# A hybrid SSD and attention layer: decay matrices by one maximum and biased exponentials, group-norm inverse roots on one row through DRAM

## Chip, cores and metric

The kernel runs on one core of one Trainium2 chip. The metric is device time in microseconds (us), as the median of several executions. Of a run with a profile, the profiled execution has a time of its own, and a span: the time from its first to its last recorded instruction. Engines are TensorE (PE), VectorE (DVE), ScalarE (ACT), GpSimd (POOL) and SyncE (SP, which here only issues transfers).

## What is computed

One inference step of one decoder layer for a prompt of 512 tokens and 8 samples of 8 new tokens each, 576 columns in all, with model width 2048. One input projection feeds two branches: a Mamba-2 mixer (causal convolution, chunked scan with decays, a SiLU gate and a grouped RMS norm) and sliding-window attention. Two gated output projections, a last projection and a final norm follow. The change touches the mixer's decay matrix and its grouped norm. For each of 8 groups of 8 heads and each chunk of 128 tokens, with `acs` the running sum of dt times A (A is negative):

```
L[s, t] = exp(acs[t] - acs[s])   for s <= t, else 0
y       = (C B^T * L) x + state part + D x
g       = y * silu(z)
out     = g * rsqrt(mean over the group's 512 channels of g*g + eps) * w
```

The kernel keeps columns as tokens and partitions as channels, so the mean over channels is a sum over partitions, taken by a matmul with a matrix of ones: each of its 128 result rows is the same.

## The kernel before

Every projection is made of **columns**: 128 output channels by 576 tokens, over 16 blocks of 128 inputs. Weights and inputs are split in a high and a low float32r part, and three products are summed (`step` in `run_main`, line 333): 16 x 3 x 2 = 96 matmuls of 128x288 for a column. The weights of half a column arrive as one 128x1024 tile (`raw`, line 68, on SP's queue), ScalarE copies the high part (`wh`, line 75), and VectorE subtracts the low part (`wl`, line 76). A column's sum stands in PSUM; two such buffers exist, so a third column can only start when the first has been copied out by its `take` function.

The mixer is worked off in 8 groups, each of six convolution columns and one mix column. `take_conv` copies a finished column to SBUF with three ScalarE copies (lines 809 to 811, tile `craw`), and queues `conv_job`: a scaled copy (`cacc`, 825), three multiply-adds on VectorE (827), two silu passes (829, 830) and the copy of the convolution state (`co`, 836). `take_mix` (1096) applies a sigmoid to a mix column. With the last x column of a group, `ssd_job(g)` is queued (872 to 978). It forms the decay matrices with `lmat` (855 to 866), multiplies them by C B^T (870), forms the scaled inputs `xe`, `xd` (900) with their high part `xh` (903, ScalarE) and low part `xl` (904, POOL), runs four chunks and then the sample tokens (`ssd_sample`), and ends with the gate and the grouped norm: the squares are summed on POOL into `tot` (957, 959), `tot` is split in `th` (963, ScalarE) and `tl` (964, POOL), the matrix of ones sums over partitions (969), ScalarE takes the root (970), VectorE the reciprocal (971) and four multiplications (975), and SP stores `y_d` (977).

```
        for s in range(2):
            ps = bank()
            for i, t_ in enumerate((th, tl)):
                ten.matmul(ps[:, :TH], ones, t_[:, s * TH:(s + 1) * TH], start=i == 0, stop=i == 1)
            act.activation(sqr[:, s * TH:(s + 1) * TH], ps[:, :TH], AF.Sqrt, bias=eps, scale=1.0 / 512)
        vec.reciprocal(sqr, sqr)
```

The jobs are Python generators. After each block of a column, `pump` runs the next step of the queued jobs, and `wait(n)` lets n such steps pass. That gives the order in which the program is written. The order in which each engine executes is then set by a scheduler that runs ahead of time, on estimated durations: so an edit in one place can move instructions in others. On the chip each engine works off its own list in that fixed order and waits for what an instruction needs.

After the mixer, the attention branch's output is read back (`stg` from `o_d`, line 1242, SP), split by ScalarE and VectorE (`ah`, `al`, 1250 and 1251), and the columns of its output projection follow. In between, `fw` (1318) and `res` (1289) are loaded.

Of the kernel before, what the change touches and what calls it, by code (L numbers as in the profile page):

```python
# [10 lines left out]
F32 = mybir.dt.float32  # L11
F32R = mybir.dt.float32r
AF = mybir.ActivationFunctionType
ALU = mybir.AluOpType
PSUM = bass.MemoryType.PSUM

P = 128
# [5 lines left out]
NS = NB * NQ  # L23
T = NP_TOK + NS
TH = T // 2
DI = 4096
H = 64
G = 8
# [27 lines left out]
def AP(t, off, dims):  # L56
    return bass.AP(t.tensor, t.offset + off, [list(d) for d in dims])
# [23 lines left out]
def hybrid(ctx, tc, x_prompt, x_sample, cache_k, cache_v, state_conv, state_ssm, norm_w, w_in, conv_w,  # L81
# [5 lines left out]
    ten, vec, act, pool, sync = nc.tensor, nc.vector, nc.scalar, nc.gpsimd, nc.sync  # L87
# [18 lines left out]
    def scratch(shape, name):  # L106
        return dram.tile(shape, F32, tag=name, name=name)
# [10 lines left out]
    xb_d = scratch([D // 2, TH], "xb_d")  # L118
    oh_d = scratch([HEADS * BL], "oh_d")
    ea_d = scratch([H, T], "ea_d")  # L120
    acs_d = scratch([H, T], "acs_d")
    e4_d = scratch([H, 4], "e4_d")
    e8_d = scratch([H, 8], "e8_d")

    def pers_tile(shape, name):
        return pers.tile(shape, F32, tag=name, name=name)
# [7 lines left out]
    eps = pers_tile([P, 1], "eps")  # L134
    sinkb = pers_tile([P, HEADS], "sinkb")
    sinks_s = pers_tile([P, 4], "sinks_s")
    dt_n = pers_tile([P, 5, H], "dt_n")
    dtd_n = pers_tile([P, 5, H], "dtd_n")
    acs_n = pers_tile([P, 5, H], "acs_n")
    cd_b = pers_tile([P, H, 4], "cd_b")  # L140
    dec_s = pers_tile([P, 32, 8], "dec_s")
    ones = pers.tile([P, P], F32R, tag="ones", name="ones")
# [22 lines left out]
    for b in order:  # L165
        if b in (0, 1):
            c0 = OFF_MA + b * P
# [87 lines left out]
    now = {}  # L255
# [45 lines left out]
    def wait(n):  # L301
        for _ in range(n):
            yield
# [441 lines left out]
    def dt_job(dtT, bt):  # L745
        x_, s, s2, p_, rst = (t[:H] for t in (dtT, cten("s"), cten("s2"), cten("p"), cten("rst")))
        sync.dma_start(out=rst, in_=c_reset)

        act.activation(s, x_, AF.Abs)
        act.activation(s, s, AF.Exp, scale=-1.0)  # L750
        tc.keep_in_program_order(act.activation(bt[:, 1:2], bt[:, 1:2], AF.Exp))
        vec.tensor_scalar(out=p_, in0=s, scalar1=2.0, scalar2=None, op0=ALU.add)
        vec.reciprocal(p_, p_)
        vec.tensor_tensor(out=s, in0=s, in1=p_, op=ALU.mult)
        vec.tensor_tensor(out=s2, in0=s, in1=s, op=ALU.mult)
        vec.tensor_scalar(out=p_, in0=s2, scalar1=2.0 / 17.0, scalar2=None, op0=ALU.mult)
        for n in (15, 13, 11, 9, 7, 5, 3):
            vec.scalar_tensor_tensor(out=p_, in0=p_, scalar=2.0 / n, in1=s2, op0=ALU.add, op1=ALU.mult)
        vec.scalar_tensor_tensor(out=p_, in0=p_, scalar=2.0, in1=s, op0=ALU.add, op1=ALU.mult)
        vec.scalar_tensor_tensor(out=x_, in0=x_, scalar=0.0, in1=p_, op0=ALU.max, op1=ALU.add)  # L760
        yield

        vec.tensor_scalar(out=s, in0=x_, scalar1=bt[:, 1:2], scalar2=-1.0, op0=ALU.mult, op1=ALU.mult)
        vec.tensor_tensor_scan(out=s2, data0=rst, data1=s, initial=0.0, op0=ALU.mult, op1=ALU.add)
        sync.dma_start(out=acs_d, in_=s2)
        act.activation(p_, s2, AF.Exp)
        sync.dma_start(out=ea_d, in_=p_)
        e4 = now["s"].tile([H, 4], F32, tag="e4", name="e4", bufs=1)
        e8 = now["s"].tile([H, 8], F32, tag="e8", name="e8", bufs=1)
        vec.tensor_copy(e4, p_[:, 0:512].rearrange("p (c l) -> p c l", l=P)[:, :, P - 1])  # L770
        vec.tensor_copy(e8, p_[:, 512:T].rearrange("p (b q) -> p b q", q=8)[:, :, 7])
        sync.dma_start(out=e4_d, in_=e4)
        sync.dma_start(out=e8_d, in_=e8)

        for lo, hi, n in ((0, 512, P), (512, T, 8)):
            v = s2[:, lo:hi].rearrange("p (c l) -> p c l", l=n)
            o = s[:, lo:hi].rearrange("p (c l) -> p c l", l=n)
            vec.tensor_tensor(out=o, in0=v[:, :, n - 1:n].to_broadcast([H, (hi - lo) // n, n]), in1=v,
                              op=ALU.subtract)
        act.activation(s, s, AF.Exp)  # L780
        vec.tensor_tensor(out=s, in0=s, in1=x_, op=ALU.mult)
        yield from wait(14)
        for srcT, dst in ((x_, dt_n), (s, dtd_n), (s2, acs_n)):
            ps = bank()
            for b in range(4):
                ten.transpose(ps[:, b * H:(b + 1) * H], srcT[:, b * P:(b + 1) * P], ident[:H, :H])
            ten.transpose(ps[:NS, 4 * H:5 * H], srcT[:, 512:T], ident[:H, :H])
            vec.tensor_copy(dst[:, 0:4, :], ps[:, 0:4 * H].rearrange("p (b h) -> p b h", h=H))
            vec.tensor_copy(dst[:NS, 4, :], ps[:NS, 4 * H:5 * H])
            yield  # L790
        sync.dma_start(out=cd_b, in_=AP(e4_d, 0, [[0, P], [1, 4 * H]]))
        eb = kten([P, 512], "eb")
        sync.dma_start(out=eb, in_=AP(e8_d, 0, [[0, P], [1, 8 * H]]))
        for hf in range(2):
            pl = slice(64 * hf, 64 * hf + 64)
            pool.tensor_copy(dec_s[pl], eb[pl].rearrange("p (t h b) -> p t h b", h=2, b=8)[:, :, hf, :])
        yield
# [57 lines left out]
    def lmat(g, c0, n, blk, rows):  # L855
        out = []
        for q in range(2):
            l_ = kten([P, 4, P], "L")
            sync.dma_start(out=l_[:rows, :, :n], in_=AP(acs_d, (8 * g + 4 * q) * T + c0, [[0, rows], [T, 4], [1, n]]))
            for i in range(4):  # L860
                h = 8 * g + 4 * q + i
                vec.tensor_scalar(out=l_[:rows, i, :n], in0=l_[:rows, i, :n], scalar1=acs_n[:rows, blk, h:h + 1],  # L862
                                  scalar2=0.0, op0=ALU.subtract, op1=ALU.min)
            act.activation(l_[:rows, :, :n], l_[:rows, :, :n], AF.Exp)  # L864
            out.append(l_)
        return out

# [5 lines left out]
    def ssd_job(g):  # L873
# [5 lines left out]
        ps = bank([P, 4, P])  # L879
# [5 lines left out]
        ps = bank([P, 4, P])  # L885
# [7 lines left out]
        for c in range(4):  # L893
# [5 lines left out]
            for o_, w_ in ((xe, dtd_n), (xd, dt_n)):  # L899
                vec.tensor_tensor(out=o_.rearrange("p (h d) -> p h d", d=64), in0=px.rearrange("p (h d) -> p h d", d=64),  # L900
                                  in1=w_[:, c, 8 * g:8 * g + 8].unsqueeze(2).to_broadcast([P, 8, 64]), op=ALU.mult)
# [12 lines left out]
            ps = bank()  # L914
# [3 lines left out]
            if c:  # L918
                vec.tensor_tensor(out=sn.rearrange("p (h d) -> p h d", d=64), in0=st.rearrange("p (h d) -> p h d", d=64),
                                  in1=cd_b[:, 8 * g:8 * g + 8, c:c + 1].to_broadcast([P, 8, 64]), op=ALU.mult)  # L920
# [15 lines left out]
            for t in range(4):  # L936
                vec.scalar_tensor_tensor(out=xs[t][:, cs], in0=xs[t][:, cs], scalar=dsk[:, 4 * g + t:4 * g + t + 1],
                                         in1=src[:, t, :], op0=ALU.mult, op1=ALU.add)
            yield from wait(2)
        ps = bank([P, 4, P])  # L940
# [22 lines left out]
        act.activation(th, tot, AF.Copy)  # L963
        pool.tensor_tensor(out=tl, in0=tot, in1=th, op=ALU.subtract)
        yield from wait(8)
        for s in range(2):
            ps = bank()
            for i, t_ in enumerate((th, tl)):
                ten.matmul(ps[:, :TH], ones, t_[:, s * TH:(s + 1) * TH], start=i == 0, stop=i == 1)
            act.activation(sqr[:, s * TH:(s + 1) * TH], ps[:, :TH], AF.Sqrt, bias=eps, scale=1.0 / 512)  # L970
        vec.reciprocal(sqr, sqr)
        yield
        for t in range(4):
            j = 4 * g + t
            vec.scalar_tensor_tensor(out=xs[t], in0=xs[t], scalar=prm[:, 240 + j:241 + j], in1=sqr, op0=ALU.mult,
# [473 lines left out]
```

## Time and profile before

| | before |
|---|---|
| median of 3 runs | 3288.77 us (3287.61 to 3290.53) |
| profiled execution | 3288.66 us |
| its span | 3286.6 us |
| mean granted clock of TensorE | 0.984 |
| busy: TensorE, VectorE, ScalarE, GpSimd | 97%, 55%, 41%, 10% |
| SSD groups with their columns | about 1335 to 2411 us of the span |

The profiled execution lies 0.1 us from the median. In the rows below, a timeline row is a start, a duration, the engine, the line of the code, the operation, the tiles it writes and reads, and in brackets how long the engine stood idle before it and what it then waited for. Matmuls that follow each other are shown as groups, and a group may end later than the next one starts.

### The profile page before, as it was taken

To read this page: it belongs to the slowest core of one execution; us is meant where nothing else is said; L and a number is where in the kernel's file an instruction comes from. 1 tells how busy PE (TensorE), PEld (TensorE's weight loads), DVE (VectorE), ACT (ScalarE), POOL (GpSimd) and SP (SyncE) were. 2 spreads that over 40 slices of the span, in tenths; PEclk is the share of its full clock that TensorE was granted. 3 is DMA by queue.
4 is the path that set the end of the run, shared out by engine and by line. 5 is a ranking of instruction groups with operands and counts; after the bars stand their busy time and mean duration, and the time that the engine had idled before them with its cause. 6 is when DMAs were issued, how large, how long until landed. Compare 5 with 4: busy or idle time off the path is not lost. (4 is left out here: it accounts for less than half of the span.)

```text
span 3286.6 us, 57410 instructions
## 1 busy us (share of the span) xinstructions
PE 3191.1 (97%) x23323; PEld 3025.2 (92%) x23323; DVE 1791.6 (55%) x3290; ACT 1336.9 (41%) x2335; POOL 332.1 (10%) x443
## 2 busy tenths in 40 slices
PE   7989999999999999999999999999979999999997
PEld 6989999999988988989899898888869999999997
DVE  7666666622644444376786776766742242423554
ACT  5434444422445546345454445444531121211443
POOL 3200000000010110112212121121110000000111
PEclk9999999999999999999999999999989999999999
DMA  6564444433333243354554544645573353533555
GB/s 201 146 152 121 120 130 116 118 104 91 94 110 94 88 122 105 94 144 129 142 151 130 155 123 126 167 111 139 153 237 105 107 163 106 149 105 96 156 163 162
DMA packets 696823, 429.17 MB, mean 131 GB/s; under 512 B 39600, under 2 KB 661952, under 8 KB 696368
## 3 DMA queue, kind: packets, MB, share of 16 engines
q1 hardware_dynamic: 668000, 397.50, 43.5%
q10 hardware_dynamic: 15552, 15.93, 1.5%
q0 software_dynamic: 13008, 12.09, 1.4%
q8 instruction: 183, 3.00, 0.4%
q14 instruction: 80, 0.66, 0.1%
HBM read 361.00 MB, written 74.67 MB: 133 GB/s over the span
## 5 line engine op out<-in xcount | busy, mean ns | idle before, releaser
L333 PE MATMUL ps<-ah,wh 128*128 128x288 f32 (+2 forms) x5408 | 1235.7, 300 | 29.0 <-ACT craw L811 16.5
L333 PE MATMUL ps<-ah,wl 128*128 128x288 f32 (+2 forms) x5408 | 1231.9, 300 | 2.0 <-DVE wl L76 1.7
L333 PE MATMUL ps<-al,wh 128*128 128x288 f32 (+2 forms) x5408 | 1232.3, 299 | 0.0
L75 ACT ACTIVATE wh<-raw 128x1024 fp32r<-128x1024 f32 x538 | 570.0, 1060 | 1305.0 <-PE ps L333 866.4
L76 DVE TENSOR_TENSOR wl<-raw,wh 128x1024 fp32r<-128x1024 f32 x538 | 670.0, 1246 | 705.0 <-ACT wh L75 697.2
L333 PEld LDWEIGHTS ps<-ah,wh 128*128 128x128 f32 x5408 | 896.8, 191 | 54.5 <-issue 21.3
L333 PEld LDWEIGHTS ps<-ah,wl 128*128 128x128 f32 x5408 | 897.7, 191 | 28.4 <-issue 22.7
L333 PEld LDWEIGHTS ps<-al,wh 128*128 128x128 f32 x5408 | 898.3, 191 | 17.0 <-issue 14.5
L437 PE MATMUL ps<-ah,wh 128*128 128x288 f32 x768 | 227.7, 296 | 5.8 <-DVE w L391 5.8
L437 PE MATMUL ps<-ah,wl 128*128 128x288 f32 x768 | 228.0, 297 | 2.0 <-DVE wl L76 2.0
L437 PE MATMUL ps<-al,wh 128*128 128x288 f32 x768 | 227.6, 296 | 0.0
L827 DVE SCALAR_TENSOR_TENSOR cacc<-craw,prm,cacc 128x600 f32<-128x600 f32 x144 | 126.9, 890 | 52.0 <-ACT cacc L825 50.8
L437 PEld LDWEIGHTS ps<-ah,wh 128*128 128x128 f32 x768 | 145.4, 189 | 6.0 <-issue 6.0
L437 PEld LDWEIGHTS ps<-ah,wl 128*128 128x128 f32 x768 | 145.3, 189 | 2.5 <-DVE wl L76 2.5
L437 PEld LDWEIGHTS ps<-al,wh 128*128 128x128 f32 x768 | 145.4, 189 | 0.1
L377 DVE TENSOR_TENSOR raw<-raw 128x1024 f32<-128x1024 f32 x96 | 117.0, 1221 | 42.4 <-DMA raw<-in_w_in_dram 41.5
L1368 POOL TENSOR_TENSOR res<-res,fw 128x128 f32<-128x128 f32 (+3 forms) x35 | 31.8, 933 | 819.8 <-ACT junk L1364 787.5
L1060 DVE SCALAR_TENSOR_TENSOR s<-s,dec_s,bank 128x128 f32<-128x128 f32 x256 | 70.6, 341 | 61.0 <-PE bank L1054 61.0
L1314 DVE TENSOR_TENSOR sg<-ps,sg 128x576 f32<-128x576 f32 x32 | 24.2, 757 | 126.1 <-PE ps L333 126.1
L593 DVE CUSTOM_DVE_ANT_0 sc<-bank,bm 128x256 f32<-128x256 f32 (+1 forms) x128 | 43.8, 388 | 79.9 <-PE bank L589 71.1
L862 DVE TENSOR_SCALAR L<-L,acs_n 128x128 f32<-128x128 f32 (+1 forms) x320 | 75.0, 302 | 18.4 <-DMA L<-acs_d 18.1
L864 ACT ACTIVATE L<-L 128x512 f32<-128x512 f32 (+1 forms) x80 | 46.2, 585 | 63.7 <-DVE L L862 53.6
(503 smaller groups left out, 3617.3 us busy)
## 6 DMA issues: line engine op xcount, KB each, us to landing
raw<-in_w_in_dram SPq DMA_DIRECT2D x306, 512.0 KB
raw<-in_w_ssm_branch_dram SPq DMA_DIRECT2D x64, 512.0 KB
raw<-in_w_out_dram SPq DMA_DIRECT2D x64, 512.0 KB
L<-acs_d SPq DMA_DIRECT2D x64, 256.0 KB
s<-in_state_ssm_dram SPq DMA_DIRECT2D x64, 256.0 KB
out_dram<-s SPq DMA_DIRECT2D x64, 256.0 KB
raw<-in_w_attn_branch_dram SPq DMA_DIRECT2D x32, 512.0 KB
zs<-z_d SPq DMA_DIRECT2D x32, 288.0 KB
```

The lines of the kernel that those rows point to most:

```text
L75: pin(nc.scalar.activation(wh, raw, AF.Copy))
L76: pin(nc.vector.tensor_tensor(out=wl, in0=raw, in1=wh, op=ALU.subtract))
L333: ten.matmul(sums[i][:, s, :part.shape[1]], a[:, kk, :], part, start=(k == 0 and q == 0), stop=(k == last and q == 2))
L377: vec.tensor_tensor(out=s_[x], in0=s_[a], in1=s_[b], op=op)
L437: ten.matmul(st[p]["ps", i][:, :TH], a[:, k, :], b, start=i < 4 and k == 0 and q == 0, stop=k == 7 and q == 2, skip_group_check=i >= 4)
L593: vec.tensor_tensor_reduce(out=s_[:, i, lo:256], in0=ps[:, i, lo:256], in1=bm[j][:, i, lo:256], scale=1.0, scalar=-3e38, op0=ALU.add, op1= ...
L827: vec.scalar_tensor_tensor(out=acc[:, :600], in0=raw[:, i:i + 600], scalar=prm[:, i * 48 + j:i * 48 + j + 1], in1=acc[:, :600], op0=ALU.mu ...
L862: vec.tensor_scalar(out=l_[:rows, i, :n], in0=l_[:rows, i, :n], scalar1=acs_n[:rows, blk, h:h + 1], scalar2=0.0, op0=ALU.subtract, op1=ALU ...
L864: act.activation(l_[:rows, :, :n], l_[:rows, :, :n], AF.Exp)
L1060: vec.scalar_tensor_tensor(out=sts[i][:, t, :], in0=sts[i][:, t, :], scalar=dec_s[:, 4 * g + t, b:b + 1], in1=ps[:, v, i, :], op0=ALU.mult ...
L1314: vec.tensor_tensor(out=sq(sg), in0=ps[:, :, :TH], in1=sq(sg), op=ALU.mult)
L1368: pool.tensor_tensor(out=res[b][:, qs], in0=res[b][:, qs], in1=fw[:rows, qs], op=ALU.mult)
```

## The change

Line numbers of the new version are in brackets here. It does three things.

1. The dt job keeps the negated running sum (`nacs_d`, `nacs_n` in place of `acs_d`, `acs_n`): a factor of -1 is left out, one exponential gets a scale of -1, and a subtraction has its operands exchanged.
2. `lmat` forms exp(min(acs[t] - acs[s], 0)) in another way: one maximum over four heads, max(nacs[t], nacs[s]) with a broadcast operand, and then per head an exponential with scale -1 and the bias nacs[s]. Four VectorE passes and one ScalarE pass become one VectorE pass and four ScalarE passes. There are 64 tiles of 128 rows with 4x128 columns, and 16 of 64 rows with 4x64.
3. The end of `ssd_job`: only row 0 of the summed squares is copied (1x288, twice [974]), stored to a DRAM scratch [975], read back as a 64x9 tile `rt` [977], put through root [979] and reciprocal [980] there, stored [981], and read back broadcast over 128 partitions into `sqr` [982]. All four transfers are issued from ScalarE's queue.

```
         vec.tensor_scalar(out=s, in0=x_, scalar1=bt[:, 1:2], scalar2=None, op0=ALU.mult)
         vec.tensor_tensor_scan(out=s2, data0=rst, data1=s, initial=0.0, op0=ALU.mult, op1=ALU.add)
...
@@ lmat
-            for i in range(4):
-                h = 8 * g + 4 * q + i
-                vec.tensor_scalar(out=l_[:rows, i, :n], in0=l_[:rows, i, :n], scalar1=acs_n[:rows, blk, h:h + 1],
-                                  scalar2=0.0, op0=ALU.subtract, op1=ALU.min)
-            act.activation(l_[:rows, :, :n], l_[:rows, :, :n], AF.Exp)
+            h = 8 * g + 4 * q
+            vec.tensor_tensor(out=l_[:rows, :, :n], in0=l_[:rows, :, :n],
+                              in1=nacs_n[:rows, blk, h:h + 4].unsqueeze(2).to_broadcast([rows, 4, n]), op=ALU.max)
+            for i in range(4):
+                act.activation(l_[:rows, i, :n], l_[:rows, i, :n], AF.Exp, scale=-1.0,
+                               bias=nacs_n[:rows, blk, h + i:h + i + 1])
@@ ssd_job
-            act.activation(sqr[:, s * TH:(s + 1) * TH], ps[:, :TH], AF.Sqrt, bias=eps, scale=1.0 / 512)
-        vec.reciprocal(sqr, sqr)
-        yield
+            act.activation(sqr[0:1, s * TH:(s + 1) * TH], ps[0:1, :TH], AF.Copy)
+        act.dma_start(out=rms_d[g, 0:1, :], in_=sqr[0:1, :])
+        rt = now["s"].tile([NS, 9], F32, tag="rt", name="rt", bufs=1)
+        act.dma_start(out=rt, in_=rms_d[g, 0].rearrange("(a b) -> a b", b=9))
+        yield from wait(6)
+        act.activation(rt, rt, AF.Sqrt, bias=eps[:NS], scale=1.0 / 512)
+        vec.reciprocal(rt, rt)
+        act.dma_start(out=rms_d[g, 1].rearrange("(a b) -> a b", b=9), in_=rt)
+        act.dma_start(out=sqr, in_=AP(rms_d[g, 1], 0, [[0, P], [1, T]]))
+        yield from wait(6)
```

Because the scheduler sets the order anew, the change also moves instructions that it doesn't name. Three places follow; the numbers behind some tile names only tell tiles apart.

**The conv stretch, ScalarE.** Before, at the sixth group, where `wh` is the weight copy, `xc` the silu of a convolution and `craw` the copy of a column `ps`:

```order
L75 ACTIVATE wh_23481<-raw_23479 128x1024
L829 ACT_TABLE_LOAD
L829 ACTIVATE xc_22909<-cacc_22964 128x512
L830 ACTIVATE xc_22909<-cacc_22964 128x64
L809 ACTIVATE craw_23231<-ps_23092 128x288
L810 ACTIVATE craw_23231<-ps_23092 128x224
L811 ACTIVATE craw_23231<-ps_23092 128x8x8
L809 ACTIVATE craw_23367<-ps_23245 128x288
L810 ACTIVATE craw_23367<-ps_23245 128x224
L811 ACTIVATE craw_23367<-ps_23245 128x8x8
L75 ACTIVATE wh_23586<-raw_23584 128x1024
```

After, at the same place (`th` belongs to the group's norm):

```order
L75 ACTIVATE wh_23352<-raw_23350 128x1024
L810 ACTIVATE craw_23268<-ps_23123 128x288
L811 ACTIVATE craw_23268<-ps_23123 128x224
L812 ACTIVATE craw_23268<-ps_23123 128x8x8
L75 ACTIVATE wh_23414<-raw_23412 128x1024
L966 ACTIVATE th_23093<-tot_23002 128x576
L830 ACTIVATE xc_23116<-cacc_23148 128x512
L831 ACTIVATE xc_23116<-cacc_23148 128x64
L75 ACTIVATE wh_23518<-raw_23516 128x1024
L810 ACTIVATE craw_23404<-ps_23282 128x288
L811 ACTIVATE craw_23404<-ps_23282 128x224
L812 ACTIVATE craw_23404<-ps_23282 128x8x8
```

Before, the two column copies stand back to back behind the weight copy, the table load and the silu; after, each stands directly behind a weight copy, with another one between them. The same pattern as before's stands in three of its groups, and in none of the new list.

**The handover, TensorE.** Before, the end of the last sample job (`L848` is its last product, `L969` the norm's matmuls with `ones`); the column matmuls between them are the rest of the last column:

```order
L1077 MATMUL bank<-ident,yo 128x128 x4
L848 MATMUL bank<-L,xd 64x64 x8
L333 MATMUL ps<-ah_247,wl 128x288
L333 MATMUL ps<-ah_249,wh 128x288 x2
L333 MATMUL ps<-al_250,wh 128x288 x2
L333 MATMUL ps<-ah_249,wl 128x288 x2
L333 MATMUL ps<-ah_251,wh 128x288 x2
L333 MATMUL ps<-al_252,wh 128x288 x2
L333 MATMUL ps<-ah_251,wl 128x288 x2
L969 MATMUL bank<-th,ones 128x288 x2
L969 MATMUL bank<-tl,ones 128x288 x2
```

After, `L849` and `L973` are the same two lines. The first rows are those behind the last sample product:

```order
L849 MATMUL bank_25850<-L_25441,xd_25491 64x64 x4
L334 MATMUL ps_25828<-ah13_248,wl_25825 128x288 x2
L334 MATMUL ps_25828<-ah14_250,wh_25824 128x288 x2
L334 MATMUL ps_25828<-al14_251,wh_25824 128x288 x2
L334 MATMUL ps_25828<-ah14_250,wl_25825 128x288 x2
L334 MATMUL ps_25828<-ah15_252,wh_25824 128x288 x2
L334 MATMUL ps_25828<-al15_253,wh_25824 128x288 x2
L334 MATMUL ps_25828<-ah15_252,wl_25825 128x288 x2
L334 MATMUL ps_25980<-ah0_222,wh_25912 128x288 x2
L334 MATMUL ps_25980<-al0_223,wh_25912 128x288 x2
```

and the end of the column that begins there, `ps_25980`:

```order
L334 MATMUL ps_25980<-ah15_252,wh_25976 128x288 x2
L334 MATMUL ps_25980<-al15_253,wh_25976 128x288 x2
L334 MATMUL ps_25980<-ah15_252,wl_25977 128x288 x2
L973 MATMUL bank_26021<-th_25955,ones_102 128x288
L973 MATMUL bank_26025<-th_25955,ones_102 128x288
L973 MATMUL bank_26021<-tl_25956,ones_102 128x288
L973 MATMUL bank_26025<-tl_25956,ones_102 128x288
L334 MATMUL ps_26242<-ah0_26119,wh_26232 128x288 x2
```

13 column matmuls stood between the sample product and the norm's; now 14 and the whole 96 of `ps_25980` do.

**The round trip, ScalarE in an odd group** (groups 1, 3 and 5). Ahead of these rows stand the two row copies, the store of line 975, a conv step and the load of line 977:

```order
L979 ACT_TABLE_LOAD
L979 ACTIVATE rt<-rt,eps 64x9
L892 ACTIVATE bh<-bank 128x512
L75 ACTIVATE wh<-raw 128x1024
L830 ACT_TABLE_LOAD
L830 ACTIVATE xc<-cacc 128x512
L831 ACTIVATE xc<-cacc 128x64
L981 DMA rms_d<-rt 64x9
L982 DMA sqr<-rms_d 128x576
L906 ACTIVATE xh<-xe 128x512
L75 ACTIVATE wh<-raw 128x1024
L1107 ACT_TABLE_LOAD
```

Line 982 stands directly behind line 981, whose landing it waits for, and `xh` behind it. In the even groups the silu, a convolution step and a copy stand between the four transfers. On VectorE, the multiplications by `sqr` [986] stand ahead of the next chunk's `xe` in the odd groups, and ahead of the decay products and `wl` in the even ones.

## Rows read from the trace of the kernel before

**Rows 1.** The page, section 1: busy time, share of the span and instructions by engine.

```profile
PE 3191.1 (97%) x23323; PEld 3025.2 (92%) x23323; DVE 1791.6 (55%) x3290; ACT 1336.9 (41%) x2335; POOL 332.1 (10%) x443
```

**Rows 2.** TensorE's waits, 1300 to 2410 us: line <- releaser: total, times, longest.

```profile
PE ps L333 <- ACT craw L811: 16.5, 6, 4.6
...
PE ps L333 <- ACT mix L1096: 1.8, 1, 1.8
PE bank L897 <- ACT xc L829: 1.4, 1, 1.4
```

**Rows 3.** Single waits of TensorE, timeline (start, duration, instruction, wait before).

```profile
2026.86 0.85 PE L333 MATMUL ps<-ah,wh 128*128 128x288 f32 x2 [4.57 <-ACT craw L811]
...
2159.71 0.61 PE L333 MATMUL ps<-ah,wh 128*128 128x288 f32 x1 [3.63 <-ACT craw L811]
...
2192.54 0.53 PE L333 MATMUL ps<-ah,wh 128*128 128x288 f32 x2 [1.55 <-ACT craw L811]
```

**Rows 4.** ScalarE's timeline ahead of the second of these.

```profile
2155.85 1.06 ACT L75 ACTIVATE wh<-raw 128x1024 fp32r<-128x1024 f32 x1 [4.72 <-PE ps L333]
...
2158.90 0.39 ACT L809 ACTIVATE craw<-ps 128x288 f32<-128x288 f32 x1
```

**Rows 5.** Busy time by stretch: length, engines, granted clock, DMA share, GB/s.

```profile
2110.00:2240.00 130.00, 124.83 (x894) 111.47 (x894) 88.37 (x175) 59.20 (x106) 23.49 (x32) 0.97 0.49 130
2160.00:2165.00 5.00, 5.00 (x22) 5.00 (x22) 0.00 (x0) 0.32 (x2) 4.84 (x6) 0.50 0.36 105
2193.00:2200.00 7.00, 7.00 (x55) 7.00 (x54) 1.38 (x3) 3.66 (x6) 1.57 (x3) 1.00 0.84 227
2432.00:2438.00 6.00, 5.70 (x23) 5.70 (x24) 6.00 (x8) 4.94 (x9) 0.00 (x0) 0.50 0.98 329
2438.00:2450.00 12.00, 12.00 (x91) 12.00 (x91) 9.68 (x14) 5.18 (x7) 0.00 (x0) 0.99 0.74 260
```

**Rows 6.** The handover, timelines of TensorE, SP and ScalarE.

```profile
2424.09 0.85 PE L969 MATMUL bank<-th,ones 128*128 128x288 f32 x2 [13.02 <-ACT th L963]
...
2432.30 0.85 PE L333 MATMUL ps<-ah,wh 128*128 128x288 f32 x2 [1.11 <-ACT mix L1096]
...
2415.35 4.39 SPq L1242 DMA_DIRECT2D stg<-o_d  x2
...
2426.83 0.68 ACT L1250 ACTIVATE ah<-stg 128x576 fp32r<-128x576 f32 x1 [0.83 <-DMA stg<-o_d]
```

**Rows 7.** Groups by line and shape: count, busy us, mean ns, idle before.

```profile
L862 DVE TENSOR_SCALAR L<-L,acs_n 128x128 f32<-128x128 f32 x256 | 61.2, 304 | 18.2 <-DMA L<-acs_d 18.1
L904 POOL TENSOR_TENSOR xl<-xe,xh 128x512 fp32r<-128x512 f32 x32 | 49.6, 1549 | 196.4 <-ACT xh L903 183.2 <-ACT craw L820 8.3 <-PE ps L333 4.5
...
L870 DVE TENSOR_TENSOR L<-L,cb 128x512 f32<-128x512 f32 x64 | 42.1, 681 | 0.0
...
L864 ACT ACTIVATE L<-L 128x512 f32<-128x512 f32 x64 | 39.8, 629 | 60.9 <-DVE L L862 51.0 <-issue 6.2 <-POOL g L823 2.1
...
L971 DVE RECIPROCAL sqr<-sqr 128x576 f32<-128x576 f32 x8 | 30.0, 3753 | 5.7 <-ACT sqr L970 5.7
...
L975 DVE SCALAR_TENSOR_TENSOR xc<-xc,prm,sqr 128x576 f32<-128x576 f32 x32 | 24.0, 813 | 0.0
...
L903 ACT ACTIVATE xh<-xe 128x512 fp32r<-128x512 f32 x32 | 20.2, 632 | 38.6 <-DVE xe L900 38.6
...
L605 ACT ACTIVATE sc<-sc,nm 128x128 f32<-128x128 f32 x32 | 12.4, 389 | 3.4 <-DVE nm L600 3.4
```

**Rows 8.** Transfers: KB, us to landing; and an L load from issue to use.

```profile
sinks_s<-sink_d POOLq DMA_DIRECT2D x2, 1.0 KB, 2.3
...
sink_d<-sk POOLq DMA_DIRECT2D x1, 1.0 KB, 3.1
...
1415.11 1.04 SPq L859 DMA_DIRECT2D L<-acs_d  x2
...
1419.84 0.68 DVE L862 TENSOR_SCALAR L<-L,acs_n 128x128 f32<-128x128 f32 x3 [2.93 <-DMA L<-acs_d]
```

More of the change, by code (lines that the diff above doesn't have):

```diff
@@ L120, in hybrid @@
     ea_d = scratch([H, T], "ea_d")
-    acs_d = scratch([H, T], "acs_d")
+    nacs_d = scratch([H, T], "nacs_d")
     e4_d = scratch([H, 4], "e4_d")
     e8_d = scratch([H, 8], "e8_d")
+    rms_d = scratch([G, 2, T], "rms_d")
     def pers_tile(shape, name):
@@ L138, in hybrid @@
     dtd_n = pers_tile([P, 5, H], "dtd_n")
-    acs_n = pers_tile([P, 5, H], "acs_n")
+    nacs_n = pers_tile([P, 5, H], "nacs_n")
     cd_b = pers_tile([P, H, 4], "cd_b")
@@ L761, in dt_job @@
         yield
-        vec.tensor_scalar(out=s, in0=x_, scalar1=bt[:, 1:2], scalar2=-1.0, op0=ALU.mult, op1=ALU.mult)
+        vec.tensor_scalar(out=s, in0=x_, scalar1=bt[:, 1:2], scalar2=None, op0=ALU.mult)
         vec.tensor_tensor_scan(out=s2, data0=rst, data1=s, initial=0.0, op0=ALU.mult, op1=ALU.add)
-        sync.dma_start(out=acs_d, in_=s2)
-        act.activation(p_, s2, AF.Exp)
+        sync.dma_start(out=nacs_d, in_=s2)
+        act.activation(p_, s2, AF.Exp, scale=-1.0)
         sync.dma_start(out=ea_d, in_=p_)
@@ L777, in dt_job @@
             o = s[:, lo:hi].rearrange("p (c l) -> p c l", l=n)
-            vec.tensor_tensor(out=o, in0=v[:, :, n - 1:n].to_broadcast([H, (hi - lo) // n, n]), in1=v,
+            vec.tensor_tensor(out=o, in0=v, in1=v[:, :, n - 1:n].to_broadcast([H, (hi - lo) // n, n]),
                               op=ALU.subtract)
@@ L782, in dt_job @@
         yield from wait(14)
-        for srcT, dst in ((x_, dt_n), (s, dtd_n), (s2, acs_n)):
+        for srcT, dst in ((x_, dt_n), (s, dtd_n), (s2, nacs_n)):
             ps = bank()
@@ L858, in lmat @@
             l_ = kten([P, 4, P], "L")
-            sync.dma_start(out=l_[:rows, :, :n], in_=AP(acs_d, (8 * g + 4 * q) * T + c0, [[0, rows], [T, 4], [1, n]]))
+            sync.dma_start(out=l_[:rows, :, :n], in_=AP(nacs_d, (8 * g + 4 * q) * T + c0, [[0, rows], [T, 4], [1, n]]))
+            h = 8 * g + 4 * q
+            vec.tensor_tensor(out=l_[:rows, :, :n], in0=l_[:rows, :, :n],
+                              in1=nacs_n[:rows, blk, h:h + 4].unsqueeze(2).to_broadcast([rows, 4, n]), op=ALU.max)
             for i in range(4):
-                h = 8 * g + 4 * q + i
-                vec.tensor_scalar(out=l_[:rows, i, :n], in0=l_[:rows, i, :n], scalar1=acs_n[:rows, blk, h:h + 1],
-                                  scalar2=0.0, op0=ALU.subtract, op1=ALU.min)
-            act.activation(l_[:rows, :, :n], l_[:rows, :, :n], AF.Exp)
+                act.activation(l_[:rows, i, :n], l_[:rows, i, :n], AF.Exp, scale=-1.0,
+                               bias=nacs_n[:rows, blk, h + i:h + i + 1])
             out.append(l_)
```

## The prediction

> **What bounds the kernel now.** I read the page first: TensorE is busy for 97% of the span, VectorE for 55%, ScalarE for 41% [rows 1]. So what an edit takes from VectorE or ScalarE is worth nothing by itself; the time changes only where TensorE stands still or runs slowly. The second view is therefore TensorE's waits over the eight SSD groups, the stretch in which the order of TensorE's instructions changes [rows 2]. The column matmuls wait 16.5 us in all for ScalarE's copies of a finished column (line 811, six times), 1.8 us for a mix column and 1.4 us for the silu: 19.7 us together. The third view, the individual waits, shows that three of the six last 4.57 and 3.63 us (one more of 3.63 at 2292.7) and the rest 1.55 us [rows 3]. The fourth shows why the long one arises [rows 4]: ScalarE's weight copy (line 75) stands ahead of the column copies and can only start when TensorE frees a buffer, which takes 4.72 us; then come a table load and the silu, and line 809 starts 3.05 us after the weight copy did. Meanwhile TensorE has filled both column buffers. The order fence for the conv stretch shows the same pile, and that the two column copies stand back to back there.
>
> The fifth view is the table by stretch [rows 5]. After the 3.63-us wait TensorE runs at a granted clock of 0.50 (the 1.2 GHz level): 22 matmuls in 5.00 us, where the full clock does 91 in 12.00 us, 0.132 us each. That is 5.00 - 22 x 0.132 = 2.1 us lost on top of the wait. After a 1.55-us wait the clock stays at 1.00.
>
> The last view is the handover from the SSD groups to the attention branch [rows 6]. TensorE waits 13.02 us for the grouped-norm matmuls, because POOL and ScalarE form `tot` and `th` behind the last sample job; then it goes in jerks, the last a wait of 1.11 us at 2432.30, and from 2432 to 2438 it runs at 0.50 [rows 5].
>
> **The change, part by part.** The sum is made against the profiled execution, 3288.66 us; the median of the three runs is 3288.77, so the two can be taken as one. A difference of 0.2% (6.6 us) is about what a measurement of this kernel can tell from nothing.
>
> *Negated decay in the dt job.* One swapped subtraction and a scale on an exponential: the same instruction counts, 0 us.
>
> *Decay matrix.* Per 128-wide tile four subtractions (304 ns each) become one maximum over 512 columns, nearest the 681 ns of the 128x512 product; one exponential of 629 ns becomes four with a bias, 389 ns each by the biased exponential of the attention part [rows 7]. VectorE gains about 64 x (1.22 - 0.68) = 34 us, ScalarE pays at most 64 x (1.56 - 0.63) = 59 us. ScalarE's total would be 1396 us of 3287, still 42%, and the job has many columns of matmuls around it, so I take 0 on TensorE's path. If that cover failed in one tile of eight, it would cost about 8 x 0.9 = 7 us.
>
> *Reciprocal.* Eight passes of 3753 ns go from VectorE [rows 7], 30 us, off the path: 0 us.
>
> *Order of the column copies.* This is a side effect that I only see in the order. The fences show that the pair of column copies behind table load and silu is gone: each copy now has its own place behind a weight copy. Going through ScalarE's list against TensorE's for all eight groups, I find none of the three long waits, none of the three of 1.55 us, and neither the mix nor the silu wait. That removes 19.7 us of waits [rows 2] and three half-clock stretches. Those are 2.1 us at least by the stretch from 2160, and 6.00 - 23 x 0.132 = 3.0 us by the one from 2432 [rows 5]; I take 2.5 each. Together -27 us, with bounds of -15 (other waits of the same kind appear) and -29.
>
> *Handover.* Before, 13 column matmuls stand between the last sample product and the norm matmuls, 13 x 0.132 = 1.7 us, and 13.0 us are waited: the chain takes 14.7 us. After, a whole further column is kept back: 14 + 96 = 110 matmuls or 14.5 us. So the 13.0-us wait is covered almost entirely. What is late next is the staging load from `o_d`: before, it was issued at 2415.35 and the first split of it came at 2426.83, 11.5 us later, with the DMA engines at 0.98 [rows 5, 6]. It stands behind one more raw weight load now. So the jerks and the half-clock stretch stay, and a few us of queueing may come. I take -11 us, with bounds of -13 and -5.
>
> *The round trip of the norm row.* Added per group: two one-row copies, then four transfers, each of which waits for the one before: row to DRAM, DRAM to the 64x9 tile, tile back, broadcast to 128 partitions. They are issued from ScalarE's queue, so a wait for a landing holds up ScalarE. Nearest rows: a 1-KB store to DRAM lands after 3.1 us, a 1-KB load after 2.3 us [rows 8]; the broadcast resembles the L load (256 KB), issued at 1415.11 and used at 1419.84, 4.7 us, at best 2.3 like the small load. Square root and reciprocal of 64x9 elements are under 0.4 us each by the 389-ns row. In the odd groups (1, 3, 5) the fence shows line 981, directly behind it 982, then `xh`. Counted from the norm matmuls: copies 0.8, store 3.1, load 2.3; the weight copy, table load and silu between put line 981 at about 11 us, 982 at 14, and the broadcast lands at 16.4 to 18.7. TensorE has 98 column matmuls (13.0 us) and about 1.6 us of transposes before it wants `xh`: 14.6 us. `xh` (632 ns) follows 982, and its remainder on POOL takes 1549 ns [rows 7]: about 1 us late. VectorE's four multiplies by `sqr` (813 ns each) stand ahead of the next chunk's `xe`, wanted at 20.5: about 2.6 us late, and a half-clock stretch of some 1.8. That is 5.4 us for each of three groups, 16 us. In the even groups 161 column matmuls (21.4 us) stand there; 1 us each for four, 4 us. In all +20 us; bounds +3 (everything but the first lateness is covered) and +40 (twice that). In the last group the trip runs beside the attention columns: 0, at worst 3 us.
>
> The Trainium skill (DMA: Bandwidth & Descriptors, "Anatomy of one DMA") gives each transfer a fixed cost of about 2.0 us, mostly the confirmation of the write. With 2.0 us in place of 3.1 and 2.3, the odd groups would lose perhaps 3 us and not 5.4, and the sum would come out 8 us lower; the traced 3.1 us decides.
>
> **Sum.** -27 - 11 + 20 = -18 us: 3288.66 - 18 = **3271 us**.
>
> **Rivals.**
> *B, the trips are hidden.* If the transfers land at the short end and the job's other slack covers them, +20 becomes +3 and the sum is -35 to -41, about 3250 us. For it: ScalarE is idle over half the time. Against it: 981 and 982 stand back to back.
> *C, cancelled.* The column waits go, but the trips cost 32 us and the handover is bound by its loads: -27 - 5 + 32 = 0, about 3289 us. For it: 0.98 of the DMA's time at the handover; the order is computed ahead of time, so ScalarE's real lateness can make new pile-ups of the same kind.
> *D, slower: the trips stall every group.* Mechanism: each of the four transfers takes the long end, 4.7 us, because the queues carry weights meanwhile (half of the DMA engines' time is taken in these stretches, 0.49 in 2110 to 2240 [rows 5]). Against 3.1 + 2.3 + 3.1 + 3.3 that is some 7 us more per group; ScalarE is held before `xh` and VectorE before `wl`, and all seven groups stop TensorE for 9 to 11 us with half-clock stretches: 70 us - 38 = +32, about 3320 us. It decides from 38 / 7 = 5.4 us per group on.
> The Trainium skill speaks for D (same page, "Rules for kernel authors"): issue a DMA early, compute, and wait late; line 982 does the contrary, being issued directly behind the store it must wait for. The same page's "Latency and other measured facts" has DRAM accesses at 0.2 us on average and 2 us under high load; no trace here shows a small store beside the weight stream, which is why D keeps a chance.
> *E, the change doesn't do what it says.* Everything said of the order rests on the listed order; if the waits in it fell elsewhere, no gain would come. That is part of C.
>
> **How the numbers follow.** Forecast, both gains kept and the trips partly paid: 3256 to 3282 us, 0.58. B 0.12, C with E 0.16, D 0.14. Faster by over 0.2% is the forecast and B, 0.70; within it C, 0.16; slower D, 0.14. The range takes in the forecast and C (up to 3295) and half of B (down to 3248): 0.80.
>
> **What would show it.** Right: no wait of the column matmuls for line 811's successor above 1 us between 1850 and 2400; no 13-us wait at the last norm matmuls; waits of 1 to 5 us for `xh`, `xl` or `xe` in odd groups, some 15 to 21 us after that group's norm matmuls; the small store landing in about 3 us. Wrong: waits for `wl` in even groups and trips of over 18 us from copy to `sqr` (D), no such waits at all (B), or new waits for column copies elsewhere (C).

## The result, and the profile after

| | before | after |
|---|---|---|
| median | 3288.19 us (3287.34 to 3290.53, 4 runs) | 3262.65 us (3258.75 to 3268.21, 4 runs) |
| ratio to before | | 0.9922 [0.9904, 0.9941] |
| profiled execution | 3288.66 us | 3258.75 us |
| its span, mean granted clock | 3286.6 us, 0.984 | 3257.0 us, 0.990 |

The change makes the kernel 25.5 us (0.8%) faster by the medians; 18 had been forecast. The two profiled executions are 29.9 us apart, and the changed kernel's runs scatter over 9.5 us, those of before over 3. On a second chip (run 5 below) the changed kernel took 3255.78 us against 3285.93, 30.2 us less (ratio 0.9905 [0.9891, 0.9920]).

The page's first section shows that the engines' totals moved the way that had been worked out, though less far: VectorE has 48 us less, where 34 and 30 had been counted, and ScalarE 46 us more, where 59 at most had been. TensorE's busy time fell by 14.5 us, though its matmuls are the same 23323; the mean granted clock rose from 0.984 to 0.990.

```profile
PE 3176.6 (98%) x23323; PEld 3009.8 (92%) x23323; DVE 1743.3 (54%) x3050; ACT 1382.7 (42%) x2581; POOL 342.8 (11%) x443
```

TensorE's waits from 1335 to 2480 us (line, what it waited for, total, times, longest), the kernel after:

```profile
PE bank L849 <- DVE L L873: 8.1, 4, 3.0
PE ps L334 <- DVE mrg L1323: 3.6, 1, 3.6
PE ps L334 <- ACT ah L1261: 3.1, 1, 3.1
PE bank L919 <- POOL xl L907: 1.7, 2, 1.0
PE bank L1077 <- ACT sT L1058: 1.1, 3, 0.5
PE bank L973 <- ACT th L966: 1.0, 1, 1.0
PE bank L1065 <- DVE xr L996: 1.0, 1, 1.0
PE bank L973 <- POOL tl L967: 0.9, 1, 0.9
PE bank L915 <- DVE st L924: 0.8, 2, 0.6
```

The three entries of [rows 2] are gone, for the copies of a column, the mix and the silu: 19.7 us. The wait of 13.02 us at the norm's matmuls [rows 6] became 1.0 and 0.9 (`th`, `tl`). New is most of the first entry, the decay product of line 873, 8.1 us: one of its four, 1.51 us at 1427.58, is ahead of the first norm, where before had 2.59 us too, and the other three (2.99, 1.36 and 2.22 us) lie some 30 us behind the norm's matmuls of the second, fourth and sixth group; and 3.6 us for `mrg`, 36 us behind the last norm matmuls. All that the view lists adds up to 21.3 us; the same view of the kernel before gives 40.2. So 19 of the 30 us are waits that went. The rest is the clock, which the table by stretch shows for the whole of 1335 to 2480 us (columns as in [rows 5]; before, then after):

```profile
1335.00:2480.00 1145.00, 1104.86 (x8019) 1001.64 (x8018) 766.50 (x1514) 532.23 (x917) 207.33 (x272) 0.98 0.53 144
```

```profile
1335.00:2480.00 1145.00, 1123.58 (x8234) 1019.48 (x8232) 726.25 (x1280) 583.77 (x1168) 220.38 (x274) 0.99 0.55 149
```

In the same 1145 us TensorE was busy 18.7 us longer, and it got 215 matmuls further, by the 0.132 us of the prediction 215 x 0.132 = 28.4 us of work at the full clock. So, as an estimate, some 10 us came from running faster while busy. The number of matmuls in this stretch is a handy measure below, since the work that lies in it is nearly the same for all versions.

**The round trip**, in the second group, seen in ScalarE's timeline (ACTq rows are issues of transfers):

```profile
1650.20 0.67 ACT L974 ACTIVATE sqr<-bank 1x288 f32<-1x288 f32 x2
1650.91 0.24 ACTq L975 DMA_DIRECT2D rms_d<-sqr  x1
...
1654.11 0.48 ACTq L977 DMA_DIRECT2D rt<-rms_d  x1
...
1657.06 0.30 ACT L979 ACTIVATE rt<-rt,eps 64x9 f32<-64x9 f32 x1 [0.86 <-DMA rt<-rms_d]
...
1657.63 0.46 ACTq L981 DMA_DIRECT2D rms_d<-rt  x1
1657.74 1.05 ACT L75 ACTIVATE wh<-raw 128x1024 fp32r<-128x1024 f32 x1
1658.81 1.28 ACT L830 ACT_TABLE_LOAD   x1
1659.29 0.33 ACTq L982 DMA_DIRECT2D sqr<-rms_d  x1
...
1661.88 0.63 ACT L906 ACTIVATE xh<-xe 128x512 fp32r<-128x512 f32 x1 [1.00 <-DVE xe L903]
...
1665.91 0.65 ACT L1107 ACTIVATE mix<-ps 128x576 f32<-128x576 f32 x1
```

and the VectorE multiplications that wait for its end:

```profile
1657.39 0.21 DVE L980 RECIPROCAL rt<-rt 64x9 f32<-64x9 f32 x1 [0.34 <-ACT rt L979]
...
1662.82 1.68 DVE L986 SCALAR_TENSOR_TENSOR xc<-xc,prm,sqr 128x576 f32<-128x576 f32 x1 [0.38 <-DMA sqr<-rms_d]
```

From the first row copy until the broadcast was used it took 1662.82 - 1650.20 = 12.6 us, where 16.4 to 18.7 had been worked out; in the other two odd groups it took 12.6 and 12.3, in the even ones 14.4 to 14.6, and in the last group 22.4. The row's store took 3.2 us until the load behind it was issued, the load 2.95 until line 979 ran, the store of 64 rows 1.66, the broadcast 3.5. And `xh` at 1661.88 waited for VectorE and not for the transfers: line 982 held nothing up.

**What the odd groups wait for instead** is seen in SP's timeline of that group, then VectorE's, then TensorE's:

```profile
1664.52 1.78 SPq L988 DMA_DIRECT2D y_d<-xc  x3
1666.59 0.32 SPq L1108 DMA_DIRECT2D ms_d<-mix  x1
1667.00 0.41 SPq L988 DMA_DIRECT2D y_d<-xc  x1
1667.47 1.45 SPq L860 DMA_DIRECT2D L<-nacs_d  x2
1669.02 0.56 SPq L68 DMA_DIRECT2D raw<-in_w_in_dram  x1
1669.62 2.13 SPq L854 DMA_DIRECT2D ea<-ea_d  x2
```

```profile
1672.20 0.69 DVE L863 TENSOR_TENSOR L<-L,nacs_n 128x512 f32<-128x512 f32 x1 [2.15 <-DMA L<-nacs_d]
...
1679.01 0.69 DVE L934 TENSOR_TENSOR ea<-bank,ea 128x512 f32<-128x512 f32 x1 [3.90 <-DMA ea<-ea_d]
1679.61 0.68 DVE L873 TENSOR_TENSOR L<-L,cb 128x512 f32<-128x512 f32 x1
```

```profile
1680.35 0.66 PE L849 MATMUL bank<-L,xd 128*64 128x128 f32 x8 [2.99 <-DVE L L873]
```

SP's rows keep the order of its list. The four `y_d` stores wait for VectorE's multiplications, and the mix store (1108) for the mix copy, whose last row above ends at 1666.56. Only then come the loads of the next chunk's decay rows (860) and, behind a weight load, of its `ea` rows (854). Issued at 1669.62, the `ea` rows are used at 1679.01; over these 9.4 us the DMA engines were busy for 0.95 of the time. On VectorE the second decay product of the chunk (873, at 1679.61) stands behind the multiplication that waits for them (934), and TensorE waits 2.99 us for it. The same order of three products (two stand at 1657.52 for the chunk before), the multiplication and the next product is found on VectorE in all eight groups; TensorE waits for a product only in the four (the first and the three odd places) in which VectorE stood idle before that multiplication, for 1.6 to 3.9 us.

### The profile page after: what moved, and what is told of

Its sections match the earlier page's. It is cut to its first block, busy times and chain, and to the rows that moved or that the text cites. A ratio compares the mean times of both kernels' runs of the same rounds, so it can differ in the third digit from the quotient of the medians.

```text
span 3257.0 us, 57475 instructions
## 1 busy us (share of the span) xinstructions
PE 3176.6 (98%) x23323; PEld 3009.8 (92%) x23323; DVE 1743.3 (54%) x3050; ACT 1382.7 (42%) x2581; POOL 342.8 (11%) x443
## 5 line engine op out<-in xcount | busy, mean ns | idle before, releaser
L334 PE MATMUL ps<-al,wh 128*128 128x288 f32 (+2 forms) x5408 | 1218.8, 298 | 0.0
L334 PEld LDWEIGHTS ps<-al,wh 128*128 128x128 f32 x5408 | 890.5, 190 | 14.5 <-issue 13.0
L866 ACT ACTIVATE L<-L,nacs_n 128x128 f32<-128x128 f32 (+1 forms) x320 | 96.2, 379 | 68.5 <-DVE L L863 68.0
L594 DVE CUSTOM_DVE_ANT_0 sc<-bank,bm 128x256 f32<-128x256 f32 (+1 forms) x128 | 43.8, 388 | 79.6 <-PE bank L590 72.0
L907 POOL TENSOR_TENSOR xl<-xe,xh 128x512 fp32r<-128x512 f32 x32 | 47.5, 1483 | 225.4 <-ACT xh L906 207.8
```

The lines of the kernel that those rows point to most:

```text
L334: ten.matmul(sums[i][:, s, :part.shape[1]], a[:, kk, :], part, start=(k == 0 and q == 0), stop=(k == last and q == 2))
L594: vec.tensor_tensor_reduce(out=s_[:, i, lo:256], in0=ps[:, i, lo:256], in1=bm[j][:, i, lo:256], scale=1.0, scalar=-3e38, op0=ALU.add, op1= ...
L866: act.activation(l_[:rows, i, :n], l_[:rows, i, :n], AF.Exp, scale=-1.0, bias=nacs_n[:rows, blk, h + i:h + i + 1])
L907: pool.tensor_tensor(out=xl, in0=xe, in1=xh, op=ALU.subtract)
```

## The experiments

Two theories stood at first. **Theory 1**: the gain is the new order of the instructions, and the norm edit alone causes it. **Theory 2**: the gain is VectorE's time, to which both edits add. Where not said otherwise, ratios are to the kernel before on the same chip, which took 3285.6 to 3285.9 us there.

**1. The decay edit alone.** The end of `ssd_job` is put back:

```
-            act.activation(sqr[0:1, s * TH:(s + 1) * TH], ps[0:1, :TH], AF.Copy)
-        act.dma_start(out=rms_d[g, 0:1, :], in_=sqr[0:1, :])
...
+            act.activation(sqr[:, s * TH:(s + 1) * TH], ps[:, :TH], AF.Sqrt, bias=eps, scale=1.0 / 512)
+        vec.reciprocal(sqr, sqr)
+        yield
```

> The negated running sum and the new decay matrix (one maximum, four biased exponentials) alone; the grouped norm ends as before. Theory 1 (the gain is the order of the instructions, and the order is set anew by the norm edit alone): the listed order still has the two column copies back to back behind weight copy, table load and silu in three groups, and one column less ahead of the last norm matmuls; so the waits of 3.6 to 4.6 us behind the column copies and the wait of about 13 us at the handover are back, and the time is 3288 us, between 3282 and 3295. Theory 2 (the gain is VectorE's time, 34 us of it from the decay matrix and 30 from the reciprocal): about half of the gain, 3275 us.

3284.91 us, ratio 1.0000 [0.9990, 1.0009]: no change. The waits, same view:

```profile
PE ps L333 <- ACT craw L811: 15.2, 6, 3.6
PE bank L971 <- ACT th L965: 10.2, 1, 10.2
```

The column-copy waits are as before (16.5 there), and the wait for `th` is 10.2 us. VectorE's time is 25 us lower in this stretch (741.30 against 766.50 us), and it bought nothing. So theory 2, in which both edits add, falls.

**2. The norm edit alone**: `lmat` and the dt job are those of before, the end of `ssd_job` is the new one.

> The norm row through DRAM alone; decay matrices and dt job as in the kernel before. Theory 1: the whole gain or slightly more, 3255 to 3265 us, no wait above 1 us for a column copy, no 13-us wait at the last norm matmuls. Theory 2: half of it, 3275 us.

3249.55 us, ratio 0.9891 [0.9874, 0.9907]: the whole gain, and more than the full change gives. The three middle stretches in which the changed kernel still lost (257.01, 257.91 and 254.92 us busy out of 260) are full here:

```profile
1590.00:1850.00 260.00, 260.00 (x1905) 232.17 (x1904) 186.08 (x388) 129.79 (x233) 53.53 (x70) 1.00 0.55 148
1850.00:2110.00 260.00, 260.00 (x1922) 234.24 (x1921) 187.77 (x389) 130.66 (x232) 54.04 (x69) 1.00 0.54 147
2110.00:2370.00 260.00, 259.97 (x1932) 234.28 (x1931) 183.84 (x386) 126.78 (x211) 57.83 (x61) 1.00 0.55 153
```

So the round trip costs TensorE nothing from 1590 to 2370 us, and the decay edit, which is worth nothing alone, takes some 6 us from the gain when it is added (3255.78 in run 5). The intervals of these two ratios overlap, but the changed kernel's idle 10 us in these three stretches are in the trace.

The loads are hardly earlier here. In the group shown they stand behind the mix store on SP (issued at 1789.40) as well, and the `ea` rows are used 9.7 us after their issue:

```profile
1791.90 1.25 SPq L854 DMA_DIRECT2D ea<-ea_d  x2
```

```profile
1800.38 1.28 DVE L871 TENSOR_TENSOR L<-L,cb 128x512 f32<-128x512 f32 x2
1801.58 0.68 DVE L932 TENSOR_TENSOR ea<-bank,ea 128x512 f32<-128x512 f32 x1
```

But on VectorE both products of the chunk stand ahead of the multiplication that needs them, in seven of the eight groups, and TensorE waits for a product only in the other one (2.5 us). In these runs a late load cost TensorE something only where the listed order put a product behind its use.

**3. The shorter reciprocal, no round trip.** Only 9 of the 576 columns get their reciprocal; for the others it is left out, so this version tells about time alone.

```
-        vec.reciprocal(sqr, sqr)
+        vec.reciprocal(sqr[:, :9], sqr[:, :9])
```

> The kernel before with the reciprocal taken of 9 of 576 columns only (the other inverse roots are left out: those columns are multiplied by the root); no transfer is added, nothing else is changed. Theory 1: the order has no pile-up of column copies and one column more ahead of the last norm matmuls, as in the changed kernel, and there is no round trip to pay: 3288 - 20 (copies, mix and silu waits) - 7 (half clock) - 11 (handover) = 3250 us, between 3243 and 3258. Theory 2: the 30 us of VectorE alone, some 13 us: 3275 us. If the transfers were wholly hidden (theory 3), this time equals that of the norm edit alone within 3 us; if they cost what I forecast (20 us), it is 15 us or more below it.

3277.20 us, ratio 0.9976 [0.9966, 0.9987]. This was a miss: the pile-ups of column copies are gone, as listed, but only 8 us came of it. The waits show why: another one took their place, for the decay product (870), and it stands in every group.

```profile
PE bank L848 <- DVE L L870: 20.4, 10, 3.2
```

**4. Logarithm and exponential in place of root and reciprocal.**

```
-            act.activation(sqr[:, s * TH:(s + 1) * TH], ps[:, :TH], AF.Sqrt, bias=eps, scale=1.0 / 512)
-        vec.reciprocal(sqr, sqr)
+            act.activation(sqr[:, s * TH:(s + 1) * TH], ps[:, :TH], AF.Ln, bias=eps, scale=1.0 / 512)
+        act.activation(sqr, sqr, AF.Exp, scale=-0.5)
```

> The kernel before with the inverse root taken as exp(-0.5 ln(x/512 + eps)) on all 128 partitions: ScalarE's two passes of 128x288 now take the logarithm, one pass of 128x576 the exponential, VectorE's reciprocal of 3753 ns is gone, and no transfer is added. Theory 1: the listed order is that of the run with the short reciprocal but for one more table load and pass on ScalarE per group, so 3250 us, between 3243 and 3260, faster than both kernels. Theory 2: 3275 us.

3275.86 us, ratio 0.9968 [0.9955, 0.9981]: a miss of the same kind. There are 20.8 us of waits for the product in nine places. SP's timeline around one of them (mix store, decay rows, weights, `ea` rows), and VectorE's behind it:

```profile
1800.54 0.36 SPq L1097 DMA_DIRECT2D ms_d<-mix  x1
1800.95 1.73 SPq L859 DMA_DIRECT2D L<-acs_d  x2
1802.78 0.45 SPq L68 DMA_DIRECT2D raw<-in_w_in_dram  x1
1803.28 1.28 SPq L853 DMA_DIRECT2D ea<-ea_d  x2
```

```profile
1810.30 0.69 DVE L931 TENSOR_TENSOR ea<-bank,ea 128x512 f32<-128x512 f32 x1 [1.89 <-DMA ea<-ea_d]
1810.90 0.68 DVE L870 TENSOR_TENSOR L<-L,cb 128x512 f32<-128x512 f32 x1
```

The mix copy ended at 1800.52, and the store of it was issued in the same moment; the loads of the next chunk stood behind it. It is the picture of the odd groups above, here without any `y_d` store in the way. That gave **theory 4**: what is left is SP's queue, in which loads stand behind stores that wait for a result. (Theory 3, in the expectation of run 3, was that the transfers are wholly hidden. Its test, run 3 against run 2, came to nothing, since run 3 had waits of its own; run 2 shows them hidden from 1590 to 2370 us, but not at the handover, where TensorE waits 3.7 us for `mrg`.)

**5 to 8, measured together on one chip.** Run 5 is the changed kernel again. Run 6 moves the mix store, run 7 the `y_d` store as well; run 8 moves the mix store in the kernel of run 4.

```
# runs 6, 7 and 8, take_mix
-            sync.dma_start(out=dst[n * P:(n + 1) * P, :], in_=t_)
+            act.dma_start(out=dst[n * P:(n + 1) * P, :], in_=t_)
# run 7, end of ssd_job
-            sync.dma_start(out=y_d[j * P:(j + 1) * P, :], in_=xs[t])
+            pool.dma_start(out=y_d[j * P:(j + 1) * P, :], in_=xs[t])
```

> The changed kernel once more, beside the next three on one chip: 3255 to 3268 us, and in the odd groups waits of 1 to 3 us for the second decay product of chunk 1 (8 us in all).

> The changed kernel with the stores of the mix rows issued from ScalarE's queue and not from SP's; the listed order of TensorE, VectorE and ScalarE stays as in the changed kernel. Theory 4 (the waits left in the odd groups come from SP's queue: the loads of the next chunk's decay rows and ea rows stand behind the four y stores, which wait for the row that came back through DRAM, and behind the mix store): the y stores still stand there, the last one 0.3 us behind the mix, so the loads start at most 0.5 us earlier and the waits stay, 6 to 8 us; time as the changed kernel within 3 us. Rival (the mix store alone holds the loads): the waits go, 8 to 10 us faster.

> The changed kernel with the mix stores on ScalarE's queue and the y stores on GpSimd's. Theory 4: nothing on SP waits for the norm or the mix any more, so the loads start earlier; the waits for the second decay product fall from 8 us to under 2, and the time falls by 6 to 10 us to about 3251. Rival (the four exponentials on ScalarE make the product late, not the loads): the waits stay and so does the time.

> The kernel with logarithm and exponential and no round trip, with the mix stores on ScalarE's queue. There the waits for the decay product are 21 us in nine places, and the y stores are long done: only the mix store stands ahead of the loads on SP. Theory 4: the waits fall under 5 us and the time from 3276 to 3252 to 3262 us. Rival: another cause (VectorE's own order); no change.

| run | median, us | ratio [95%] | waits for the product, us | matmuls in 1335 to 2480 |
|---|---|---|---|---|
| 5, changed kernel | 3255.78 | 0.9905 [0.9891, 0.9920] | 8.6 | 8234 |
| 6, mix store moved | 3257.30 | 0.9908 [0.9893, 0.9923] | 8.0 | 8211 |
| 7, both stores moved | 3245.65 | 0.9873 [0.9857, 0.9890] | none listed | 8321 |
| 8, run 4 with mix store moved | 3236.77 | 0.9846 [0.9831, 0.9860] | none listed | 8381 |

All four came as theory 4 has it, run 8 by more than it said (39 us below run 4, which was measured on another chip, where 14 to 24 were expected). The expectation counted the waits for the product, 20.8 us; all that the view lists fell from 39.1 us in run 4 to 10.6, and TensorE got 314 matmuls further in the stretch, about 41 us at 0.132 each. In run 6 the order of the other engines is that of the changed kernel, and nothing moved: the `y_d` stores still stood ahead. In run 7, in the same group, SP issued the decay rows at 1658.97 and not at 1667.47, before the norm row had come back:

```profile
1658.97 1.18 SPq L860 DMA_DIRECT2D L<-nacs_d  x2
...
1666.27 2.18 SPq L854 DMA_DIRECT2D ea<-ea_d  x2
```

In run 8 the decay rows were issued 4.4 us ahead of the mix copy (SP, then ScalarE):

```profile
1781.97 1.12 SPq L859 DMA_DIRECT2D L<-acs_d  x2
```

```profile
1786.39 0.65 ACT L1096 ACTIVATE mix<-ps 128x576 f32<-128x576 f32 x1
```

TensorE's waits in run 8, all that are listed from 1335 to 2480 us:

```profile
PE ps L333 <- ACT ah L1250: 4.8, 1, 4.8
PE ps L333 <- ACT mix L1096: 3.3, 1, 3.3
PE bank L916 <- POOL xl L904: 1.5, 1, 1.5
PE bank L1066 <- ACT sT L1047: 1.0, 1, 1.0
```

One reservation: taking a store off SP lets the scheduler lay out the lists anew. Of the instructions that VectorE executed from 1335 to 2480 us, 99.8% stand in the same sequence in run 6 as in the changed kernel, but 92% in run 7, and 92% in run 8 as in run 4. So in these two an earlier load and another order came together, and no run has the one without the other. An order held fixed by hand was not tried. What speaks for the load is the place of the wait itself, three products, the multiplication by `ea` and the next product. In runs 4 and 8 this order stands in all eight groups. In run 4 VectorE was idle before the multiplication for 1.7 to 4.0 us in every group; in run 8 for at most 1.8, here 1.14, which TensorE did not notice:

```profile
1794.01 0.69 DVE L931 TENSOR_TENSOR ea<-bank,ea 128x512 f32<-128x512 f32 x1 [1.14 <-DMA ea<-ea_d]
1794.62 0.68 DVE L870 TENSOR_TENSOR L<-L,cb 128x512 f32<-128x512 f32 x1
```

In run 7 the order is kept in two of the three odd places. In the one whose SP rows stand above, the next product moved ahead of the multiplication, so there the order alone could have removed the wait.

**9 and 10, the controls.** Run 9 moves the mix store in the kernel before; run 10 adds the decay edit to run 8.

> The kernel before with the mix stores on ScalarE's queue, nothing else. Its listed order keeps the two column copies back to back behind weight copy, table load and silu, now in four groups. If the queue alone made the gain of the run with logarithm and exponential, this gains 30 us too, 3250 us. By theory 1 the pile-ups and the 13-us wait at the handover stay: 3280 to 3295 us.

> The fastest kernel so far (logarithm and exponential, mix stores on ScalarE's queue) with the negated sum and the new decay matrix added. If ScalarE's 42 us of further exponentials cost something of their own, TensorE waits for the decay products again, and the time rises by 5 us or more. If the decay edit only mattered through SP's queue (theory 4), the time stays within 4 us of 3237.

Run 9: 3286.41 us, ratio 1.0007 [0.9997, 1.0016], with 20.7 us of column-copy waits and the 13.0 us at the handover. The queue alone gives nothing while the pile-ups stand. Run 10: 3238.36 us, ratio 0.9855 [0.9839, 0.9872], which is run 8 within the runs' scatter, with no wait for a product. So the four exponentials cost nothing that these runs can tell: with the loads early, the decay edit is neither a gain nor a loss.

Run 8 is the fastest version: 3236.77 us, 49 us below the kernel before and 19 below the changed one, without the DRAM round trip.

## Why the prediction held, and where it was off

The sum was -27 - 11 + 20 = -18 us; measured were -25.5 by the medians of the first measurement, -29.9 by the profiled executions. The odd groups' waits and their half-clock stretch came to some 7.6 us (below); with that in place of 20 the same sum gives -30.

- *Parts costed at nothing.* The maximum took 692 ns (681 assumed) and a biased exponential 390 (389). Neither moved TensorE by itself: run 1. The 34 us of VectorE's gain were too many, since they multiply means: by [rows 7] the 256 subtractions of 304 ns were busy for 61.2 us and not for 78, as passes overlap, and the 64 maxima for 43.8, so this edit freed some 17 us there.
- *Column copies, -27.* The 19.7 us of waits went entirely, in the way the order had shown, and the half-clock stretches with them. The granted clock from 1850 to 2370 us is 1.00 now, against 0.98.
- *Handover, -11.* The waits there fell from 16.6 us (13.02, 0.63, 1.15, 0.65, 1.11) to 8.7 (1.04, 0.95, 3.12, 3.58), and the half-clock stretches shrank with them; no run sets this gain apart from the rest, so the -11 is not measured by itself. What was late next is what had been named: the staging load, 3.12 us for `ah`. The 3 us allowed at worst for the last group's round trip came as well, 3.58 us at 2432.54: line 986 waited for `sqr` until 2421.48, the `y_d` stores went out at 2422.33, and the loads of `sg` behind them on SP came 4.88 us late for `mrg`. A wait of 3.5 to 5.2 us for `mrg` is listed in all four versions with the round trip (the changed kernel, runs 2, 6 and 7), and in none without it.
- *Round trips, +20.* This is the term that was wrong, in size and place. The odd groups were to lose 5.4 us each because line 982 would hold up `xh` on ScalarE and line 986 `xe` on VectorE. They lost 2.99, 1.36 and 2.22 us (and one half-clock stretch), 6.6 us where 16 had been put, and the clock some 1 us more (28 matmuls in 4.65 busy us from 1680 to 1685); in the even groups no such wait stands. The trip was shorter, 12.6 us, since line 981 did not wait for the weight copy ahead of it in the list, and what it delayed was neither `xh` nor `xe`, but the stores on SP and through them the loads of the next chunk, which the decay edit's new order on VectorE then turned into waits (run 2 has the trips and not these waits). The prediction had followed what stands behind the transfers on ScalarE's and VectorE's lists, and not what the later `y_d` stores hold up on SP's.
- *Rivals.* B's mechanism (the trips are hidden) is right for the norm edit alone from 1590 to 2370 us: run 2. D's four long trips did not occur: 3.2, 2.95, 1.66 and 3.5 us.
- *What the prediction did not see*: that the two edits do not add. The norm edit alone gives 36 us, the decay edit 0, both together 30. That the total still came near the forecast is partly luck: the odd groups did lose time, but by another path than the one worked out.

The Trainium skill (DMA: Bandwidth & Descriptors, "Anatomy of one DMA") gives a transfer, on the path from GpSimd that it describes, a fixed 2.0 us or so. Of the three small transfers in the group shown, issued from ScalarE, only the 64-row store was below that (1.66 us); the row's store and the load took 3.2 and 2.95 us, near the traced 3.1 us of [rows 8]. Neither figure holds everywhere: in the third group of run 2 the load behind the same row store was issued 1.2 us after it (1770.91 and 1772.13). The Trainium skill's rule to issue early and wait late (same page, "Rules for kernel authors") fits a place I had not applied it to: in the changed kernel TensorE waited not for the round trip, but for the chunk's loads behind the stores (2.99, 1.36 and 2.22 us), and in run 7, with these loads issued earlier, no such wait is listed.

## What to carry to other kernels

When a scheduler sets the order ahead of time, a small edit's worth can lie wholly in the instructions it moves elsewhere: compare the lists of the engines, and test each edit alone, since two edits' gains need not add. A queue that issues in order should not carry loads behind stores that wait for a result, at least where the consumer's list puts urgent work behind such a load; look at what stands ahead of a late load, not only at how long it takes. And a gap that closes uncovers the next: after each removed wait, the list of waits is read again.

## What was not expected of the hardware

ScalarE's transfers ran ahead of its passes, so the fixed order told of above does not hold for the start times of a transfer and a pass. In the list, line 981 stands behind the weight copy, a table load and two silu passes; in the trace it was issued at 1657.63, as soon as the reciprocal was done, 0.11 us before that weight copy began, and line 982 at 1659.29, during the table load listed ahead of it. A wait for a landing did not always pass unnoticed, though: in four of the groups line 831 waited about 1 us (4.2 us in all, 1.07 in the first) for the landing of line 975's store, which line 977 ahead of it needs. And two loads of 128 KB, issued at 1669.62 behind a weight load and two of 256 KB, were used 9.4 us later with the DMA engines at 0.95 over that time, while the first of two of 256 KB issued at 1667.47 was used after 4.7 us, as in [rows 8], with the DMA engines at 0.92.
